# Gated linear attention in a two-layer trunk: one stacked product per chunk and head

## The chip, the cores and the metric

The kernel runs on one core of a Trainium2 chip. The metric is the device time of one execution in microseconds (us). Before the change the median of three runs is 723.94 us (723.78 to 724.06).

## The reference

Two layers over one sequence of 256 positions with 1024 features, in float32. Each layer multiplies by one wide matrix, gives the columns to three groups of heads, multiplies their joined outputs by `w_out`, normalises, and runs a mixture of experts (16 experts, 2 per token) with another normalisation. Groups B and C are softmax attentions with four heads of 64. Group A, which the change concerns, is gated linear attention: four heads, keys of 64, values of 128, and four chunks of 64 positions.

```
b = cumsum(log_a, axis=3)                     # within a chunk
q_dec = (q * 64 ** -0.5) * exp(b)
k_inv = k * exp(-b)
a = where(causal, einsum('bhnid,bhnjd->bhnij', q_dec, k_inv), 0)
o_intra = einsum('bhnij,bhnjv->bhniv', a, v)
kv = einsum('bhncd,bhncv->bhndv', k * exp(b_last - b), v)
S_in[n + 1] = decay[n] * S_in[n] + kv[n]      # S_in[0] = 0
o = o_intra + einsum('bhncd,bhndv->bhncv', q_dec, S_in)
o = rms_norm(o, norm_gain) * silu(g_out)
```

So per head and chunk the output is masked scores times values plus decayed queries times the state that the chunk starts with.

## The kernel before

The 256 positions are two tiles of 128 (`t`), each of two chunks. A layer's mixer begins with the projection `pj`: the transposed input and each weight tile are split into a high and a low half in a rounded format, and three products (`whi` with `hhi`, `wlo` with `hhi`, `whi` with `hlo`) are summed. ACT makes `whi`, DVE makes `wlo`. The column groups come in the order of `ORDER` (line 39): the indexer, values, `GV` (values and gate rank of the linear attention), queries and keys of the two softmax attentions, `GK`, and `GG`, the output gate. The out-projection `po` uses the same three-product form, with `mx` for the softmax attentions and `mxG` for the linear one; `OUT_ORDER` (line 40) puts the four row blocks of `mxG` last (42 products of them before the first normalisation begins).

The class `Order` with `_Lane` (from line 75 on) fixes the order of instructions while the program is built. It holds a clock for each engine, books every instruction with the duration that `_Lane.cost` returns, and runs generators: a generator yields the tiles that it waits for, or a number of PSUM banks that must be free, and goes on when the booked clock of TensorE has reached that point. In between, the backbone (projection and out-projection) fills TensorE. So another duration in `cost`, or another `yield`, moves instructions on every engine. There are eight PSUM banks; `bank` takes one and `od.free` gives it back. Weights come in a ring of 33 buffers through SP's DMA queue. `pieces.fill` makes `whi` and `wlo` a fixed number of tiles ahead.

The generators that the change edits:

- `decays` (line 862): copies the values of both tiles from PSUM to `gv` (ACT, four copies), makes the gate's cumulative sums and the exponentials `eb`, `enb`, `ebl`.
- `linear` (line 939): `qd` is the decayed queries, `enb` and `ebl` become the two decayed keys. For each tile: four products `aT` (keys by queries, 64 rows of contraction), and a masked copy into `aM`, which was zeroed. Four transposes of `ebl` through TensorE give `kd`, which one ACT copy evicts. For each of three chunks: four products `kv`, and the state `S` (ACT's copy for the first, DVE for the others). For each tile and head the output bank gets a product of `aM` with `gv` over 128 rows, and one or two products of `qd` with `S` over 64 rows. Then ACT squares, DVE sums (`ms`), POOL takes the power -0.5, and DVE multiplies (`og`).

Two generators that run beside these are not edited but are moved: `softmax_pv` (line 602) with the scores `sc`, their maxima on DVE, the exponentials `s_sb` on ACT, the division by `ri` on DVE, transposes `pT`, products `pv` and the split into `mx`; and `gated` (line 1072), which multiplies `og` by `sg` (silu of the gate, ACT), transposes it (`tr` from `og`), and evicts the high half (ACT) and the low half (DVE) of `mxG`. Every instruction goes through one helper, so nearly all rows carry one line, L235 in the kernel before and L237 in the changed one.

Of the kernel before, what the change touches and what calls it, by code (L numbers as in the profile page):

```python
# [17 lines left out]
P = 128  # L18
# [13 lines left out]
SENT = -3e38  # L32
THETA = 500000.0
TWO_PI = 2.0 * math.pi
CHUNKS = {"I": ([(3088, 584)], (1,) * 8, (292, 292)), "GV": ([(512, 528)], (1,) * 8, (264, 264)),
# [151 lines left out]
class _Lane:  # L187
# [3 lines left out]
    def cost(self, name, out, ins, kw, scalars=0):  # L191
        def free(a):
            n = 1
            for s in a.shape[1:]:
                n *= s
            return n
        n = free(out)
        psum = any(i.space == bass.MemoryType.PSUM for i in ins)
        if self.lane == "PE":
            if name == "transpose":  # L200
                return 110.0
            f = 1.68 if ins[0].dtype == F32 else 0.42
            c = max(214.0 if ins[0].dtype == F32 else 100.0, f * n)
            return c / 2 + 20 if out.shape[0] <= 64 and ins[0].shape[0] > 64 else c
        if self.lane == "ACT":
            return 0.833 * n + (52 if psum else 94) + 93 * (scalars + ("accum_out" in kw))
        if self.lane == "POOL":
            if name == "memset":
                return 0.8 * n + 70
            return 165.0 * n + 300 if kw.get("op") == OP.pow else 2.2 * n + 50  # L210
        m = max([n] + [free(a) for a in ins])
        if name == "reciprocal":
            return 6.3 * n + 68
        if name in ("tensor_scalar", "tensor_copy") and not psum:
            return 0.54 * n + 65 + 61 * scalars
        return 1.04 * m + 65 + 61 * scalars
# [23 lines left out]
def trunk_kernel(ctx, tc, x, positions, w_in, gate_up, gate_bias, norm_gain, w_out, ln_mix_g, ln_mix_b,  # L240
# [503 lines left out]
    for l in range(DEPTH):  # L744
# [114 lines left out]

        gl = {}  # L860

        def decays(ps):
            rT = t1("rT", (17, L))
            pool.memset(rT, 1.0)
            gv, ranks = [], []
            for t in range(NT):
                r_ = sm("rank", 16)
                act.activation(r_, ps[t][1][:, 248:264], AF.Copy)
                ranks.append(r_)
                gv.append(t2("gv"))  # L870
# [4 lines left out]
            gl["v"] = gv  # L875
            yield ranks
            yield 1
            b_ = bank("tr")
# [60 lines left out]
        def linear(bq, bk):  # L939
            while "decays" not in done:  # L940
                yield lambda: "decays" in done
            eb, enb, ebl = gl["e"]
            gv = gl["v"]
            gq, gk = (b.rearrange("p (a n) -> p a n", a=2) for b in (bq, bk))
            yield [bq, bk]
            dve.tensor_mul(enb, gk, enb)
            qd = t2("qd", (P, 2, L))
# [5 lines left out]
            yield [qd, enb]  # L953
            aM = t4("aM", (P, NT, 2, 2, P))
            pool.memset(aM, 0.0)
            for t in range(NT):
                ts = slice(t * P, (t + 1) * P)
                yield 2
                b_ = [bank("aT") for _ in range(2)]
                for hh in range(4):  # L960
                    r = slice(64 * (hh % 2), 64 * (hh % 2) + 64)
                    mm(b_[hh % 2].rearrange("p (h i) -> p h i", h=4)[:, hh // 2], enb[r, hh // 2, ts],
                       qd[r, hh // 2, ts])
                yield b_
                for s_ in range(2):
                    dve.copy_predicated(aM[:, t, s_], triu.bitcast(I32)[:, None, :].to_broadcast([P, 2, P]), b_[s_].rearrange("p (h i) -> p h i", h=4)[:, 0:2])
                od.free(*b_)
            yield ebl
            yield 1
            b_ = bank("kd")  # L970
            kdp = b_.rearrange("p (t n) -> p t n", t=NT)
            for t in range(NT):
# [4 lines left out]
            od.free(b_)  # L977
            yield kd
            S = []
            for c in range(3):  # L980
                yield 1
                b_ = bank("kv")
                kv = b_.rearrange("p (a n) -> p a n", a=4)
                u = slice(64 * (c % 2), 64 * (c % 2) + 64)
                for hh in range(4):
                    mm(kv[64 * (hh % 2):64 * (hh % 2) + 64, hh // 2], kd[u, c // 2, hh * 64:hh * 64 + 64],
                       gv[c // 2][u, hh * P:(hh + 1) * P])
                yield b_
                s = t1("S", (P, 2, P))
                if c == 0:  # L990
                    act.activation(s, kv[:, 0:2], AF.Copy)
                else:
                    for a in range(2):
                        dve.scalar_tensor_tensor(s[:, a], S[-1][:, a], eb[:, a, 64 * c + 63:64 * c + 64],
                                                 kv[:, a], op0=OP.mult, op1=OP.add)
                od.free(b_)
                S.append(s)
            for t in range(NT):
                yield ([S[0]], S[1:])[t]
                yield 2  # L1000
                bs = [bank("o") for _ in range(2)]
                b3 = [b.rearrange("p (h n) -> p h n", h=4)[:, 0:2] for b in bs]
                for hh in range(4):
                    r = slice(64 * (hh % 2), 64 * (hh % 2) + 64)
                    o_ = b3[hh % 2]
                    mm(o_[:, hh // 2], aM[:, t, hh % 2, hh // 2], gv[t][:, hh * P:(hh + 1) * P],
                       start=True, stop=False)
                    for u in range(2):
# [4 lines left out]
                sq = t2("sq", (P, 2, 2, P))  # L1013
                ms = sm("ms", 12)
                yield bs
                for s_ in range(2):
                    act.activation(sq[:, s_], b3[s_], AF.Square)
                yield sq
                dve.tensor_reduce(ms[:, 0:4].rearrange("p (a b) -> p a b", a=2), sq, AX.X, OP.add)
# [4 lines left out]
                for s_ in range(2):  # L1024
                    dve.tensor_mul(o[:, s_::2], b3[s_],
                                   ms[:, 8 + 2 * s_:10 + 2 * s_][:, :, None].to_broadcast([P, 2, P]))
                od.free(*bs)
                og.append(o)
            done.add("og")

# [662 lines left out]
```

## Time and profile before

| | us |
|---|---|
| median of three runs | 723.94 |
| the profiled execution | 723.8 |
| its span | 722.1 |
| TensorE (PE) busy | 692.0 (96%) |
| VectorE (DVE) busy | 440.7 (61%) |
| ScalarE (ACT) busy | 269.1 (37%) |
| GpSimd (POOL) busy | 44.0 (6%) |

The span runs from the first to the last instruction in the trace. PE's busy time counts products only; loads of weights (PEld) run beside them. An instruction of TensorE in float32 appears twice per product, a transpose once: `o<-S,qd ... x4` is two products. In a name such as `aT<-qd,enb` the tile left of the arrow is written, those right of it are read. Busy time of an engine that others wait for matters; idle time of the others does not.

### The profile page before, as it was taken

Reading aid. Unit: us, or ns where it says so; the run is one execution under the profiler, and the core shown is the slowest. Engines: PE = TensorE matmul, PEld = TensorE weight load, DVE = VectorE, ACT = ScalarE, POOL = GpSimd, SP = SyncE. Lnnn points to the kernel's source line nnn. Section 1 sums busy time; section 2 is a strip of 40 time slices with the busy share of each in tenths; the row PEclk is TensorE's granted clock in tenths of the full one; section 3 lists DMA queues with packets and bytes.
Section 4 is the critical chain, followed back from the end, with each engine's and each line's share of the span. In section 5 each row is a group of like instructions: output and inputs, shape, how many; then the busy total and the mean of one; then the engine's idle time right before and its main releaser. Section 6 shows DMA issues by size and latency. Waiting matters only on the chain. (4 is left out here: it accounts for less than half of the span.)

```text
span 722.1 us, 11110 instructions
## 1 busy us (share of the span) xinstructions
PE 692.0 (96%) x3817; PEld 400.0 (55%) x3817; DVE 440.7 (61%) x1115; ACT 269.1 (37%) x549; POOL 44.0 (6%) x72
## 2 busy tenths in 40 slices
PE   7999999999999989999899999999999999899993
PEld 6897977853533533533488889777435334343330
DVE  5897874660635445676488688757343546259645
ACT  5668646441312112212186666464223012022121
POOL 2000001010000001200130000011000000011002
PEclk9999999999999999999999999999999999999997
DMA  9899845879999999999999755469799999999971
GB/s 307 277 391 407 337 162 190 293 264 405 409 404 408 406 407 409 408 409 408 356 391 401 276 176 174 147 214 344 262 409 408 403 407 408 405 409 409 408 295 58
DMA packets 83245, 243.01 MB, mean 337 GB/s; under 512 B 10148, under 2 KB 14312, under 8 KB 83176
## 3 DMA queue, kind: packets, MB, share of 16 engines
q1 hardware_dynamic: 82504, 241.86, 88.0%
q8 instruction: 34, 0.56, 0.3%
q10 hardware_dynamic: 416, 0.26, 0.1%
q14 instruction: 35, 0.29, 0.1%
q0 software_dynamic: 256, 0.03, 0.0%
HBM read 241.08 MB, written 1.05 MB: 335 GB/s over the span
## 5 line engine op out<-in xcount | busy, mean ns | idle before, releaser
L235 PE MATMUL gu<-wf,xT 128*64 128x512 f32 x912 | 226.0, 594 | 3.7 <-PEq L1412 3.7
L235 PEld LDWEIGHTS gu<-wf,xT 128*64 128x64 f32 x912 | 71.8, 137 | 131.8 <-issue 124.1
L235 DVE SCALAR_TENSOR_TENSOR yt<-y,ws,yt 32x512 fp32r<-32x512 f32 (+1 forms) x116 | 86.7, 748 | 94.7 <-ACT yt L235 93.2
L235 DVE TENSOR_TENSOR wlo<-wf,whi 128x512 fp32r<-128x512 f32 (+2 forms) x174 | 97.3, 598 | 38.9 <-ACT whi L235 36.5
L235 PE MATMUL y<-wf,actT 128*64 128x512 f32 x432 | 110.5, 595 | 1.8 <-ACT actT L235 1.8
L235 ACT ACTIVATE whi<-wf 128x512 fp32r<-128x512 f32 (+2 forms) x176 | 86.7, 551 | 14.1 <-PE po L235 9.5
L235 PE MATMUL pj<-whi,hhi 128*128 128x512 f32 (+2 forms) x224 | 81.6, 364 | 0.0
L235 PE MATMUL pj<-wlo,hhi 128*128 128x512 f32 (+2 forms) x224 | 78.1, 349 | 1.7 <-DVE wlo L235 1.5
L235 PE MATMUL pj<-whi,hlo 128*128 128x512 f32 (+2 forms) x224 | 77.7, 347 | 0.0
L235 ACT ACTIVATE yt<-y,ws 128x512 fp32r<-128x512 f32 x60 | 36.9, 688 | 104.2 <-PE y L235 77.3
L235 PEld LDWEIGHTS y<-wf,actT 128*64 128x64 f32 x432 | 34.0, 137 | 54.1 <-issue 41.4
L235 DVE TENSOR_TENSOR act<-act,gu 128x512 f32<-128x512 f32 x16 | 11.0, 688 | 84.4 <-PE gu L235 62.8
L235 PE MATMUL gu<-wx,xT 128*64 128x512 f32 x112 | 52.7, 596 | 0.0
L235 PEld LDWEIGHTS pj<-whi,hhi 128*128 128x128 f32 x224 | 42.1, 188 | 8.3 <-issue 2.9
L235 PEld LDWEIGHTS pj<-wlo,hhi 128*128 128x128 f32 x224 | 42.1, 188 | 7.2 <-DVE wlo L235 3.5
L235 PEld LDWEIGHTS pj<-whi,hlo 128*128 128x128 f32 x224 | 42.0, 188 | 5.1
L235 ACT ACTIVATE actT<-aT 128x512 f32<-128x512 f32 x16 | 9.5, 595 | 85.8 <-PE aT L235 85.8
L235 ACT ACTIVATE xT<-xT,cols 128x256 f32<-128x256 f32 x32 | 17.4, 565 | 56.9 <-PE xT L235 56.9
L235 ACT ACTIVATE act<-gu 128x512 f32<-128x512 f32 x16 | 9.6, 597 | 76.4 <-PE gu L235 76.4
L235 PE MATMUL y<-wx,actT 128*64 128x512 f32 x80 | 33.4, 595 | 0.0
L235 DVE TENSOR_TENSOR z<-z,sc 128x512 f32<-128x512 f32 x48 | 29.7, 680 | 0.4 <-PE sc L235 0.4
L235 PE MATMUL sc<-yt,sT 128*128 128x512 f32 x72 | 23.8, 430 | 1.7 <-ACT yt L235 1.6
(269 smaller groups left out, 923.4 us busy)
## 6 DMA issues: line engine op xcount, KB each, us to landing
wf<-in_w_expert_gate_dram SPq DMA_DIRECT2D x114, 512.0 KB, 10.1
wf<-in_w_expert_up_dram SPq DMA_DIRECT2D x114, 512.0 KB, 10.0
wf<-in_w_expert_down_dram SPq DMA_DIRECT2D x108, 512.0 KB, 10.1
wf<-in_w_in_dram SPq DMA_DIRECT2D x32, 512.0 KB, 10.0
wx<-in_w_expert_down_dram SPq DMA_DIRECT2D x36, 256.0 KB, 5.8
wf<-in_w_out_dram SPq DMA_DIRECT2D x16, 512.0 KB, 10.5
wx<-in_w_expert_up_dram SPq DMA_DIRECT2D x24, 256.0 KB, 6.7
wx<-in_w_expert_gate_dram SPq DMA_DIRECT2D x10, 512.0 KB, 7.6
```

Of the source, the lines that this page charges most:

```text
L235: return fn(*a, **kw)
```

## The change

Scores and queries are stacked on the contraction rows, and so are values and states, so that a head's output in a chunk is one product over 128 rows. `X` holds, for head and chunk, the decayed queries in one half of the partitions and the masked scores in the other; `W[c]` holds the state of the chunk's start and the chunk's values in the matching halves. The halves change places between even and odd heads. The scores, `kd` and `kv` are made on 64 by 64 tiles, because they must land in the right half. The values' columns of `GV` are divided 256 and 272 in place of 264 and 264. `cost` gets one more rule for products on 64 by 64 tiles.

```diff
+            if out.shape[0] <= 64 and ins[0].shape[0] <= 64 and n <= 128:
+                return max(50.0, f * n / 2)
...
-                act.activation(gv[t][:, 0:264], ps[t][0][:, 0:264], AF.Copy)
-                act.activation(gv[t][:, 264:512], ps[t][1][:, 0:248], AF.Copy)
+            W = [t2("W", (P, 4, P)) for _ in range(4)]
+            pool.memset(W[0], 0.0)
+            for t in range(NT):
+                for u in range(2):
+                    for s_ in range(2):
+                        for a in range(2):
+                            act.activation(W[2 * t + u][half(1 - s_), 2 * a + s_], ps[t][a][half(u), s_ * P:(s_ + 1) * P], AF.Copy)
...
-            dve.scalar_tensor_tensor(qd, gq, 0.125, eb, op0=OP.mult, op1=OP.mult)
+            for s_ in range(2):
+                r = half(s_)
+                dve.scalar_tensor_tensor(X[r, s_::2].rearrange("p a c i -> p a (c i)"), gq[r], 0.125, eb[r], op0=OP.mult, op1=OP.mult)
...
+            for a in range(2):
+                for c in range(4):
+                    for s_ in range(2):
+                        mm(b4[s_][half(1 - s_), a, c], enb[half(s_), a, 64 * c:64 * c + 64], X[half(s_), 2 * a + s_, c])
+            yield bs
+            for s_ in range(2):
+                o = half(1 - s_)
+                dve.copy_predicated(X[o, s_::2], triu.bitcast(I32)[o, None, None, o].to_broadcast([64, 2, 4, 64]), b4[s_][o])
...
-            for t in range(NT):
                 for a in range(2):
-                    tr(kdp[:, t, a * P:(a + 1) * P], ebl[:, a, t * P:(t + 1) * P])
-            kd = t2("kd", (P, NT, 256))
-            act.activation(kd, kdp, AF.Copy)
+                    for s_ in range(2):
+                        mm(b4[s_][half(1 - s_), c, a], ebl[half(s_), a, 64 * c:64 * c + 64], ident[half(s_), half(s_)])
+                for s_ in range(2):
+                    act.activation(kd[c][half(1 - s_)], b4[s_][half(1 - s_), c], AF.Copy)
...
+                        mm(kv[s_][half(s_), a], kd[c][half(1 - s_), a], W[c][half(1 - s_), 2 * a + s_])
...
+                            dve.scalar_tensor_tensor(W[c + 1][r, 2 * a + s_], W[c][r, 2 * a + s_], eb[r, a, 64 * c + 63:64 * c + 64],
+                                                     kv[s_][r, a], op0=OP.mult, op1=OP.add)
...
-                    mm(o_[:, hh // 2], aM[:, t, hh % 2, hh // 2], gv[t][:, hh * P:(hh + 1) * P],
-                       start=True, stop=False)
                     for u in range(2):
-                        c = 2 * t + u
-                        if c:
-                            mm(o_[64 * u:64 * u + 64, hh // 2], qd[r, hh // 2, 64 * c:64 * c + 64],
-                               S[c - 1][r, hh // 2], start=False, stop=True)
+                        mm(b3[half(u), hh], X[:, hh, 2 * t + u], W[2 * t + u][:, hh])
...
+                act.activation(sq, b3, AF.Square)
...
+                dve.tensor_mul(o, b3, ms[:, 8:12, None].to_broadcast([P, 4, P]))
```

On TensorE, in layer 0, the output block of tile 1 stood between `pv` and the last projection products. Before:

```order
L235 MATMUL pT<-ident,s_sb 128x128 x8
L235 MATMUL pv<-pT,v 64x128 x12
L235 MATMUL o<-gv,aM 128x128
L235 MATMUL o<-S,qd 64x128 x2
L235 MATMUL o<-gv,aM 128x128
L235 MATMUL o<-S,qd 64x128 x2
L235 MATMUL o<-gv,aM 128x128
L235 MATMUL o<-S,qd 64x128 x2
L235 MATMUL o<-gv,aM 128x128
L235 MATMUL o<-S,qd 64x128 x2
```

and now, in the same place:

```order
L237 MATMUL pT<-ident,s_sb 128x128 x8
L237 MATMUL pv<-pT,v 64x128 x12
L237 MATMUL po<-whi,mx 128x512
L237 MATMUL po<-wlo,mx 128x512
L237 MATMUL po<-whi,mx 128x512 x2
L237 MATMUL po<-wlo,mx 128x512
L237 MATMUL po<-whi,mx 128x512
L237 MATMUL o<-W,X 64x128 x8
```

The twelve products of the block are eight of one form, and six products of the out-projection have come between it and `pv`.

On TensorE, in layer 1, near the end of the mixer, the transposes of `og` stood apart, among products of `po`. Before:

```order
L235 MATMUL po<-wlo,mx 128x512
L235 MATMUL po<-whi,mx 128x512
L235 MATMUL tr<-ident,og 128x128 x4
L235 MATMUL po<-whi,mx 128x512
L235 MATMUL po<-wlo,mx 128x512
L235 MATMUL po<-whi,mx 128x512 x2
L235 MATMUL po<-wlo,mx 128x512
L235 MATMUL po<-whi,mx 128x512
L235 MATMUL tr<-ident,og 128x128 x4
L235 MATMUL po<-whi,mx 128x512
```

and now:

```order
L237 MATMUL po<-wlo,mx 128x512
L237 MATMUL po<-whi,mx 128x512
L237 MATMUL tr<-ident,og 128x128 x8
L237 MATMUL pT<-ident,s_sb 128x128 x8
L237 MATMUL pv<-pT,v 64x128 x12
L237 MATMUL po<-whi,mx 128x512
L237 MATMUL po<-wlo,mx 128x512
```

The eight transposes stand together, and `pT` and `pv` of the second softmax tile, which stood ahead of the second `o` block before, stand right behind them.

On DVE, at the same place of layer 1, before:

```order
L235 TENSOR_REDUCE ms<-sq 128x4
L235 TENSOR_SCALAR ms<-ms 128x4
L235 TENSOR_TENSOR wlo<-wf,whi 128x512 x2
L235 TENSOR_TENSOR og<-o,ms 128x2x128 x2
L235 TENSOR_TENSOR og<-og,sg 128x512 x2
L235 TENSOR_TENSOR wlo<-wf,whi 128x512 x2
L235 SCALAR_TENSOR_TENSOR mxG<-tr,cols,mxG 128x4x128
L235 TENSOR_TENSOR wlo<-wf,whi 128x512
L235 SCALAR_TENSOR_TENSOR mxG<-tr,cols,mxG 128x4x128
```

and now (`ISA` is the maximum over a head's scores):

```order
L237 ISA s_sb,mx<-sc,acc 128x256
L237 ISA mx 128x1
L237 TENSOR_SCALAR mx<-mx 128x4
L237 TENSOR_TENSOR wlo<-wf,whi 128x512
L237 TENSOR_TENSOR og<-o,ms 128x512
L237 TENSOR_TENSOR og<-og,sg 128x512 x2
L237 SCALAR_TENSOR_TENSOR mxG<-tr,cols,mxG 128x4x128 x2
L237 RECIPROCAL ri<-mx 128x4
L237 TENSOR_SCALAR s_sb<-s_sb,ri 128x256 x4
L237 TENSOR_TENSOR mx<-pv,mx 128x512
```

The second softmax tile's maxima (four pairs of ISA rows, the last one shown) have come between the sum `ms` and `og`, and its scalings stand behind the two `mxG` evictions.

## Rows read from the trace of the kernel before

**Rows 1.** The page, busy us, share of the span and instructions of each engine.
```profile
PE 692.0 (96%) x3817; PEld 400.0 (55%) x3817; DVE 440.7 (61%) x1115; ACT 269.1 (37%) x549; POOL 44.0 (6%) x72
```
**Rows 2.** Windows: us, busy of PE, PEld, DVE, ACT, POOL, PEclk, DMA share, GB/s.
```profile
480.00:490.00 10.00, 10.00 (x50) 8.28 (x49) 8.03 (x14) 7.14 (x12) 0.00 (x0) 1.00 0.64 213
```
**Rows 3.** Waits of PE: us in total, times, longest us.
```profile
PE pj L235 <- DVE wlo L235: 1.5, 3, 0.7
```
**Rows 4.** Timeline of PE, layer 0: start us, us, what.
```profile
97.14 0.40 PE L235 MATMUL pj<-whi,hlo 128*128 128x512 f32 x1
97.47 0.71 PE L235 MATMUL aT<-qd,enb 64*128 64x128 f32 x8
...
98.45 0.39 PE L235 MATMUL pj<-wlo,hhi 128*128 128x512 f32 x1
98.68 0.40 PE L235 MATMUL pj<-whi,hlo 128*128 128x512 f32 x1
...
100.45 0.60 PE L235 MATMUL kd<-ident,ebl 128*128 128x128 f32 x4
...
102.36 0.65 PE L235 MATMUL kv<-gv,kd 64*64 64x128 f32 x8
```
**Rows 5.** Timeline of PE, layer 0, around the two output blocks.
```profile
107.22 0.40 PE L235 MATMUL pj<-whi,hlo 128*128 128x512 f32 x1
...
110.82 0.40 PE L235 MATMUL pj<-wlo,hhi 128*128 128x512 f32 x1
...
115.71 1.58 PE L235 MATMUL pv<-pT,v 128*64 128x128 f32 x24
117.22 0.49 PE L235 MATMUL o<-gv,aM 128*128 128x128 f32 x2
...
120.69 0.39 PE L235 MATMUL pj<-wlo,hhi 128*128 128x512 f32 x1
```
**Rows 6.** Timeline of PE, layer 1, transposes of the second softmax tile.
```profile
470.32 1.03 PE L235 MATMUL pT<-ident,s_sb 128*128 128x128 f32 x8
```
**Rows 7.** Timeline of ACT, value copies of layer 0, end of layer 1's mixer.
```profile
49.20 1.21 ACT L235 ACTIVATE gv<-pj 128x264 f32<-128x264 f32 x4
...
471.02 1.09 ACT L235 ACTIVATE pT<-pT 128x512 f32<-128x512 f32 x2 [2.54 <-PE pT L235]
472.95 0.60 ACT L235 ACTIVATE mx<-pv 128x512 fp32r<-128x512 f32 x1 [0.85 <-ACT pT L235]
...
482.16 0.69 ACT L235 ACTIVATE mxG<-tr,cols 128x512 fp32r<-128x512 f32 x1
```
**Rows 8.** Timeline of DVE, layer 1, end of the mixer.
```profile
461.81 0.42 DVE L235 CUSTOM_DVE_ANT_0 s_sb<-sc,acc 128x256 f32<-128x256 f32 x1 [1.71 <-PE sc L235]
...
466.75 0.17 DVE L235 RECIPROCAL ri<-mx 128x4 f32<-128x4 f32 x1
466.95 1.14 DVE L235 TENSOR_SCALAR s_sb<-s_sb,ri 128x256 f32<-128x256 f32 x4
...
476.54 0.69 DVE L235 TENSOR_REDUCE ms<-sq 128x4 f32<-128x512 f32 x1 [2.26 <-ACT sq L235]
...
477.46 0.69 DVE L235 TENSOR_TENSOR wlo<-wf,whi 128x512 fp32r<-128x512 f32 x1
...
479.44 0.75 DVE L235 TENSOR_TENSOR og<-o,ms 128x256 f32<-128x256 f32 x2
480.11 1.28 DVE L235 TENSOR_TENSOR og<-og,sg 128x512 f32<-128x512 f32 x2
...
482.89 0.75 DVE L235 SCALAR_TENSOR_TENSOR mxG<-tr,cols,mxG 128x512 fp32r<-128x512 f32 x1
```
**Rows 9.** Windows: a stop of PE, and the end of the span.
```profile
261.00:262.00 1.00, 0.00 (x0) 0.00 (x0) 0.00 (x0) 0.00 (x0) 0.00 (x0) 1.00 1.04 414
...
709.00:712.00 3.00, 1.46 (x4) 0.59 (x4) 2.12 (x5) 0.19 (x1) 0.15 (x1) 1.00 0.00 0
712.00:713.00 1.00, 0.00 (x0) 0.00 (x0) 0.93 (x5) 0.06 (x1) 0.55 (x2) 0.64 0.00 0
```

More of the change, by code (lines that the diff above doesn't have):

```diff
@@ L860, in trunk_kernel, with half @@
         gl = {}
+        def half(s):
+            return slice(64 * s, 64 * s + 64)
         def decays(ps):
@@ L942, in linear @@
             eb, enb, ebl = gl["e"]
-            gv = gl["v"]
+            W = gl["W"]
             gq, gk = (b.rearrange("p (a n) -> p a n", a=2) for b in (bq, bk))
+            X = t4("X", (P, 4, 4, 64))
+            for s_ in range(2):
+                pool.memset(X[half(1 - s_), s_::2], 0.0)
             yield [bq, bk]
             dve.tensor_mul(enb, gk, enb)
-            qd = t2("qd", (P, 2, L))
-            dve.scalar_tensor_tensor(qd, gq, 0.125, eb, op0=OP.mult, op1=OP.mult)
+            for s_ in range(2):
+                r = half(s_)
+                dve.scalar_tensor_tensor(X[r, s_::2].rearrange("p a c i -> p a (c i)"), gq[r], 0.125, eb[r], op0=OP.mult, op1=OP.mult)
             od.free(bq)
@@ L952, in linear @@
             od.free(bk)
-            yield [qd, enb]
-            aM = t4("aM", (P, NT, 2, 2, P))
-            pool.memset(aM, 0.0)
-            for t in range(NT):
-                ts = slice(t * P, (t + 1) * P)
-                yield 2
[L959 to L967, printed above, removed]
@@ L998, in linear @@
[L998 to L1005, printed above, removed]
-                    mm(o_[:, hh // 2], aM[:, t, hh % 2, hh // 2], gv[t][:, hh * P:(hh + 1) * P],
-                       start=True, stop=False)
-                    for u in range(2):
-                        c = 2 * t + u
-                        if c:
-                            mm(o_[64 * u:64 * u + 64, hh // 2], qd[r, hh // 2, 64 * c:64 * c + 64],
-                               S[c - 1][r, hh // 2], start=False, stop=True)
-                sq = t2("sq", (P, 2, 2, P))
-                ms = sm("ms", 12)
+            yield [X, enb]
@@ new lines, in linear @@
+            yield 2
+            bs = [bank("aT") for _ in range(2)]
+            b4 = [b.rearrange("p (a c i) -> p a c i", a=2, c=4) for b in bs]
+            for a in range(2):
[6 more added lines that the diff above has]
+                dve.copy_predicated(X[o, s_::2], triu.bitcast(I32)[o, None, None, o].to_broadcast([64, 2, 4, 64]), b4[s_][o])
@@ new lines, in linear @@
+            od.free(*bs)
+            yield ebl
+            yield 2
+            bs = [bank("kd") for _ in range(2)]
+            b4 = [b[:, 0:384].rearrange("p (c a d) -> p c a d", c=3, a=2) for b in bs]
+            kd = [t1("kd", (P, 2, 64)) for _ in range(3)]
+            for c in range(3):
+                for a in range(2):
+                    for s_ in range(2):
+                        mm(b4[s_][half(1 - s_), c, a], ebl[half(s_), a, 64 * c:64 * c + 64], ident[half(s_), half(s_)])
+                for s_ in range(2):
+                    act.activation(kd[c][half(1 - s_)], b4[s_][half(1 - s_), c], AF.Copy)
@@ L1015, in linear @@
+            od.free(*bs)
+            for c in range(3):
+                yield [kd[c], W[c]]
+                yield 2
+                bs = [bank("kv") for _ in range(2)]
+                kv = [b.rearrange("p (a n) -> p a n", a=4) for b in bs]
+                for a in range(2):
+                    for s_ in range(2):
+                        mm(kv[s_][half(s_), a], kd[c][half(1 - s_), a], W[c][half(1 - s_), 2 * a + s_])
                 yield bs
                 for s_ in range(2):
-                    act.activation(sq[:, s_], b3[s_], AF.Square)
+                    r = half(s_)
+                    if c == 0:
+                        act.activation(W[1][r, s_::2], kv[s_][r, 0:2], AF.Copy)
+                    else:
+                        for a in range(2):
+                            dve.scalar_tensor_tensor(W[c + 1][r, 2 * a + s_], W[c][r, 2 * a + s_], eb[r, a, 64 * c + 63:64 * c + 64],
+                                                     kv[s_][r, a], op0=OP.mult, op1=OP.add)
+                od.free(*bs)
@@ new lines, in linear @@
+            for t in range(NT):
+                yield [X] + W[2 * t:2 * t + 2]
+                yield 1
+                b_ = bank("o")
+                b3 = b_.rearrange("p (h n) -> p h n", h=4)
+                for hh in range(4):
+                    for u in range(2):
+                        mm(b3[half(u), hh], X[:, hh, 2 * t + u], W[2 * t + u][:, hh])
+                sq = t2("sq", (P, 4, P))
+                ms = sm("ms", 12)
+                yield b_
+                act.activation(sq, b3, AF.Square)
@@ L1018, in linear @@
                 yield sq
-                dve.tensor_reduce(ms[:, 0:4].rearrange("p (a b) -> p a b", a=2), sq, AX.X, OP.add)
+                dve.tensor_reduce(ms[:, 0:4], sq, AX.X, OP.add)
                 dve.tensor_scalar(ms[:, 4:8], ms[:, 0:4], 1.0 / P, RMS_EPS, op0=OP.mult, op1=OP.add)
@@ L1023, in linear @@
                 o = t2("og", (P, 4, P))
[L1024 to L1027, printed above, removed]
+                dve.tensor_mul(o, b3, ms[:, 8:12, None].to_broadcast([P, 4, P]))
+                od.free(b_)
                 og.append(o)
```

35 lines of the change are left out of this document (4 added, 31 removed).

## The prediction

> **What bounds the kernel now.** I read the page's busy shares first: TensorE (PE) is busy 692.0 of 722.1 us, and no other engine comes near [rows 1]. Then the busy time by windows, for the mixer: in 480:490 PE is busy all of its 10 us at clock 1.00, beside 8.03 us of VectorE (DVE) and 7.14 of ScalarE (ACT) [rows 2]; the windows around the linear attention read alike in both layers. The list of PE's waits has one entry that a mixer edit touches: 1.5 us in three waits for `wlo`, the low half of a weight, the longest 0.7 us [rows 3]. The timeline of PE then shows the blocks themselves without a gap. So the bound is PE's own instruction stream; work taken off it moves the end one for one, and so does every gap that opens in it. The MoE behind each mixer runs from PE as well and passes a shift on.
>
> **What PE sheds, per layer.** Projection products start 0.23 us apart (98.45 and 98.68). The first `aT` block: from the product at 97.14 to the second one behind it at 98.45 are 1.31 us, less two products at 0.23 is 0.85; two such blocks 1.7. The `kd` transposes have a row of 0.60, which overlaps its neighbours; I count 0.4 [rows 4]. Output block `o` of t=0: 107.22 to 110.82 is 3.60, less two products 3.1; of t=1: 117.22 to 120.69 less one is 3.2 [rows 5]. Together 1.7 + 0.4 + 6.3 = 8.4 us per layer.
>
> **What PE takes on, per layer.** (a) Scores `aT`: sixteen products on 64 by 64 tiles with 64 columns. The nearest row is `kv`: four such products with 128 columns, 0.65 us [rows 4], with the 0.14 by which a block costs more than its row (0.85 against 0.71 for `aT`) 0.8. Of its eight instructions in pairs at 0.11 us, 0.45 is streaming and 0.35 the change of tiling in and out. Sixteen products are sixteen pairs: 0.9 with half the columns, 1.75 if 64 columns cost as many as 128. So 1.2 to 2.1; I take 1.2. (b) `kd`: twelve products of the same shape, 1.0 (upper bound 1.7). Here PE stops twice for ACT, which empties each chunk's pair of banks with two copies of 64x128 before PE writes on. Four `gv` copies of 264 or 248 columns take 1.21 us, 0.27 from start to start [rows 7]; a copy of 128 columns lies between 0.15 and 0.27, with the latency of one (0.4 at most) a stop is 0.3 to 0.7; I take 0.6, so 1.2 for two. (c) `o`: eight products with all 128 rows and 64 output columns, twice. The row of that form is `pv`: 24 instructions in 1.51 us [rows 5], so sixteen in 1.0, with the change of tiling 1.23; twice 2.5. Sum 1.2 + 1.0 + 1.2 + 2.5 = 5.9. **PE sheds 2.5 us per layer** before anything waits.
>
> **What waits now, layer 0.** The sixteen ACT copies of `v` replace four: 16 times 0.15 to 0.27 against 1.21, 1.2 to 3.1 us more ahead of the weight halves `whi` in ACT's queue, and `wlo` on DVE and the projection products wait behind these. Cover is the pieces made ahead; without it all of it would show. Bounds 0 and 3.1; I take 0.7, the longest wait for `wlo` seen [rows 3]. Before, eighteen products of `po` stood between the last transposes of `og` and the first product that reads `mxG`; now the eight transposes stand directly ahead of it, and the ACT eviction of 0.69 us [rows 7] and the start of DVE's of 0.75 [rows 8] show: 0.9. `pv` is followed by `po` rather than by `o`, some 0.3 for the change of tiling. The score products and the second `o` block find their inputs ready. The other edits on DVE, ACT and POOL (zeroing, queries in two instructions, fewer masked copies, states written in halves) I cost at nothing, since projection products stand beside them; without these each would show with its own length, some 0.3 to 0.7 by the rows of like size [rows 7, 8]. SP issues the same weight transfers in the same order. Layer 0: -2.5 + 0.7 + 0.9 + 0.3 = -0.6; the `kv` blocks stand alone more often, +0.3. I take -0.3.
>
> **What waits now, layer 1.** The end of the mixer is put together differently. Everything of the second softmax (`pT`, `pv`) now stands behind the transposes of `og`, and 24 `po` products behind `pv`.
> First stop, before the `og` transposes. After `pT` of t=0 PE has eight score instructions with 256 columns (four pairs at twice 0.11, with the change of tiling 1.1) and twelve `po` products at 0.23 (2.8): 3.9 us. Beside it, from the same point: ACT's `pT` copy (0.5 after its start-up of 0.2; two take 1.09), the square over 512 columns (0.6 by the same row) [rows 7], then on DVE the reduce 0.7, a `wlo` 0.6, four score maxima of 0.42 that overlap a little (1.5), a `wlo` 0.6, `og` over 512 columns 0.65, the first `og` times `sg` 0.65 [rows 8], and 0.3 of small operations and hand-overs: 6.3. Stop 2.4 us. Without the maxima and the `wlo` in between it would be some 0.3; with a later ACT it grows one for one.
> Second stop, between those transposes and `pT` of t=1. DVE's queue has the two `mxG` evictions ahead of the reciprocal and the four scalings that `pT` reads. From the first four transposes: ACT's `mxG` 0.7 [rows 7], DVE's two 0.7 each, reciprocal 0.2, first scaling 0.35, hand-overs 0.2 [rows 8]: 2.8, less the 0.4 of the other transposes: 2.4 us. Before, the products of `po` stood there and nothing waited.
> Third, `po` behind `pv` needs `mx`: ACT's copy 0.60 [rows 7] with hand-overs 0.9, and 0.2 until DVE's half. Before, the second `o` block covered this.
> Behind them the 42 products on `mxG` find all ready. Layer 1: -2.5 + 2.4 + 2.4 + 1.1 = +3.4. Uncertainty of the three stops: 3 to 8 in all.
>
> **The clock.** It is 1.00 through the span but for the first microseconds and the tail. A PE that stood still through all of 261:262 left it at 1.00; at the tail, where four products in 709:712 were all the work, 1.46 us busy of 3, it was 0.64 in 712:713, the mean of a stretch at 2.4 and one at 1.2 GHz [rows 9]. Layer 1 would now have two stops of 2.4 us with one microsecond of transposes between: thinner than the tail before its fall. I think a fall to 1.2 GHz in the second stop likelier than not. Its least price is the eight `pT` transposes at half rate, 1.03 more [rows 6]; with `pv` too it is 2.5, and with as many `po` products as the kernel's other cold stretch, 4. I take 1.2.
> The Trainium skill, page "TensorE: Matmul & The Clock Gate", section "Why this matters for your kernels", says that idle gaps between bursts of products in the middle of a kernel send the clock back to its lower level; rows 9 show one gap that did not. [...]
>
> **Sum.** Profiled execution of before 723.8 us (span 722.1 and 1.7 around it); -0.3 + 3.4 + 1.2 = +4.3: 728.1. The median of the runs shown is 723.94, 0.14 above the profiled one; so 728.2.
> The same skill's page "TensorEngine Tiling (Array Packing)", section "PSUM Bottleneck", warns that after tiling the emptying of PSUM may become the bottleneck, and asks for evictions over many tiles at once; this change splits them. No row shows that here yet; by it the stops above are the lasting cost.
>
> **Rivals.**
> *The clock stays.* All waits as above, without 1.2: 727.0. For it speaks the gap at 261 us, against it the tail [rows 9].
> *The waits are hidden: faster.* The freed 2.5 us per layer reach the end, because the second `og` arrives in time. That needs ACT and DVE in layer 1 to run 2.4 us ahead of what I assume, ahead of the first stop, and the `mxG` evictions to be done before PE gets through its transposes. Deciding point: the first stop under 0.3 us. Then 723.9 - 5.0 + 1.9 of layer 0's waits + some 1 = 721.8. Against it: the order of DVE's queue is fixed in the program, and each of its durations is in a row.
> *The stops are half as long.* Layer 1 -2.5 + 3.0 = +0.5, layer 0 -0.3, the clock kept: 724.1, no change to be told.
> *Narrow products cost like wide ones.* `aT` 0.9 and `kd` 0.7 more in each layer (the upper bounds above), 3.2 in all, nothing of it hidden: 731.4 with the clock's fall, 730.2 without. For it: no row has 64 columns on TensorE in this form; against it, times of products follow columns from 128 to 512 in the rows.
> *The clock falls for longer.* Through `pv` and some `po`: 729.5 to 731.
>
> **How the numbers follow.** Forecast with the clock's short fall 0.34, clock kept 0.24, long fall 0.16, narrow products dear 0.10, half stops 0.09, faster 0.07. Each case has about 1 us of its own to either side. Leaving out the lowest tenth (faster, the edge of half stops) and the highest tenth: 725.0 to 731.5. About 0.2% (1.4 us) is what a measurement of this kernel can tell from no change: faster by more 0.07, within 0.10, slower 0.83.
>
> **What would show it.** In the changed kernel's trace: `aT` in one block of about 1.2 us and each `o` block of 1.2 where 3.1 stood; two gaps of PE of 2 to 3 us either side of eight `og` transposes in layer 1, the second released by DVE's scaled scores, and a third near 1 us behind `pv`; layer 0's mixer as long as before within 1 us; PEclk below 1.00 somewhere between the first gap and the `po` products behind it. The MoE stretches keep their length. I am wrong if the gaps in layer 1 stay under 2 us in sum, or if PE's blocks of narrow products take 2 us each; a mixer in layer 1 that is shorter than before refutes the forecast.

## The result and the profile after

The changed kernel takes 733.82 us (median of four runs, 732.62 to 735.40) against 723.86 for the kernel before (four runs, 723.38 to 724.06): ratio 1.0133, 95% interval 1.0119 to 1.0148. It is slower, as forecast, but by 10.0 us where 4.3 were forecast, and the time lies above the range.

The profiled execution of the changed kernel is the longest of the four, 735.4 us with a span of 733.7; it stands 11.6 us behind that of before. The page's busy row and the largest of PE's waits that a mixer can cause:

```profile
PE 695.3 (95%) x3873; PEld 402.7 (55%) x3873; DVE 444.4 (61%) x1117; ACT 278.1 (38%) x582; POOL 44.7 (6%) x76
```

```profile
PE tr L237 <- DVE og L237: 2.7, 1, 2.7
PE pT L237 <- DVE s_sb L237: 2.2, 1, 2.2
...
PE pj L237 <- DVE wlo L237: 1.8, 4, 0.8
...
PE kd L237 <- ACT kd L237: 1.2, 4, 0.4
...
PE gx L237 <- issue: 0.7, 1, 0.7
PE po L237 <- ACT mx L237: 0.7, 1, 0.7
...
PE po L237 <- ACT mxG L237: 0.3, 1, 0.3
```

Against [rows 1, 3]: PE is busy 3.3 us longer although the change takes work off it, since part of its work ran at half clock (below), and the first two waits are new. They are the two stops that the forecast named. On the timeline of PE at the end of layer 1's mixer (against [rows 6]):

```profile
480.23 0.39 PE L237 MATMUL po<-whi,mx 128*128 128x512 f32 x1
483.29 1.16 PE L237 MATMUL tr<-ident,og 128*128 128x128 f32 x8 [2.68 <-DVE og L237]
486.62 1.97 PE L237 MATMUL pT<-ident,s_sb 128*128 128x128 f32 x8 [2.16 <-DVE s_sb L237]
488.51 2.88 PE L237 MATMUL pv<-pT,v 128*64 128x128 f32 x24
492.08 0.50 PE L237 MATMUL po<-whi,mx 128*128 128x512 f32 x1 [0.69 <-ACT mx L237]
```

The eight `pT` take 1.97 us where they took 1.03, and the 24 `pv` instructions 2.88 where they took 1.58: near half rate. The windows show the clock there, and in two stretches that the forecast did not price, the routings between mixer and experts (columns as in [rows 2]):

```profile
149.00:150.00 1.00, 0.99 (x9) 0.76 (x8) 0.92 (x9) 0.47 (x3) 0.00 (x0) 1.00 1.04 383
150.00:151.00 1.00, 0.11 (x1) 0.00 (x0) 1.00 (x10) 1.00 (x1) 0.00 (x0) 0.87 1.06 387
151.00:152.00 1.00, 0.81 (x4) 0.84 (x5) 0.97 (x9) 0.14 (x1) 0.00 (x0) 0.50 1.06 389
...
157.00:158.00 1.00, 1.00 (x8) 1.00 (x7) 0.75 (x2) 0.72 (x2) 0.00 (x0) 0.72 0.00 0
...
482.00:483.00 1.00, 0.00 (x0) 0.00 (x0) 1.00 (x2) 1.00 (x5) 0.00 (x0) 1.00 0.20 25
...
486.00:487.00 1.00, 0.39 (x2) 0.39 (x3) 0.96 (x5) 0.73 (x2) 0.00 (x0) 0.50 0.59 221
...
517.00:518.00 1.00, 1.00 (x6) 0.94 (x6) 0.15 (x1) 0.00 (x0) 0.00 (x0) 0.50 0.29 119
```

PEclk, the column behind POOL, reads 0.50 (1.2 GHz) from 150.7 to 157.6, from 485.2 to 492.1 and from 516.0 to 519.4 us (the edges follow from the shares of the windows), and 1.00 between. The fall at 485 follows the stop of 2.7 us, the transposes and part of the second stop. The one at 150.7 lies in a wait of 1.08 us for DVE, behind idle products and one small product; the one at 516 lies just behind the same wait in layer 1. Both kernels have this wait. In layer 0, before and after:

```profile
151.59 1.18 PE L235 MATMUL xT<-G,h 128*128 128x128 f32 x8 [1.08 <-DVE top L235]
```

```profile
151.19 2.05 PE L237 MATMUL xT<-G,h 128*128 128x128 f32 x8 [1.08 <-DVE top L237]
```

The starts of the same instruction in both timelines show where the 11.6 us arose (`gu` is the experts' first product, `lgT` the routing's, `gq` the first of `GK`, `warm` idle products):

| until | before | after | behind | in the stretch |
|---|---|---|---|---|
| first `sc` of layer 0 | 71.61 | 71.73 | +0.12 | +0.97, less 0.85 (the clock rose at 7.4, not 9.1) |
| first `lgT` of layer 0 (mixer's end) | 146.11 | 145.72 | -0.39 | -0.51 |
| first `gu` of layer 0 | 155.65 | 158.12 | +2.47 | +2.86, routing, clock 0.50 |
| `warm` ahead of layer 1 | 356.78 | 358.93 | +2.15 | -0.32, experts |
| first `gq` of layer 1 | 432.72 | 435.82 | +3.10 | +0.95 |
| first `lgT` of layer 1 | 500.33 | 510.36 | +10.03 | +6.93 |
| first `gu` of layer 1 | 509.86 | 521.43 | +11.57 | +1.54, routing, clock 0.50 |

The blocks `aT` and `o` cost what was forecast, `kd` 0.5 us more. PE in layer 0, against [rows 4, 5]:

```profile
100.01 0.39 PE L237 MATMUL pj<-whi,hlo 128*128 128x512 f32 x1
100.33 1.15 PE L237 MATMUL aT<-X,enb 64*64 64x64 f32 x32
...
101.74 0.39 PE L237 MATMUL pj<-wlo,hhi 128*128 128x512 f32 x1
101.97 0.40 PE L237 MATMUL pj<-whi,hlo 128*128 128x512 f32 x1
102.30 0.45 PE L237 MATMUL kd<-ident,ebl 64*64 64x64 f32 x8
103.11 0.74 PE L237 MATMUL kd<-ident,ebl 64*64 64x64 f32 x8 [0.36 <-ACT kd L237]
104.10 0.74 PE L237 MATMUL kd<-ident,ebl 64*64 64x64 f32 x8 [0.26 <-ACT kd L237]
...
105.11 0.40 PE L237 MATMUL pj<-wlo,hhi 128*128 128x512 f32 x1
...
124.45 0.40 PE L237 MATMUL po<-whi,mx 128*128 128x512 f32 x1
124.78 1.09 PE L237 MATMUL o<-W,X 128*64 128x128 f32 x16
...
126.14 0.39 PE L237 MATMUL po<-wlo,mx 128*128 128x512 f32 x1
```

By the subtraction of [rows 4], `aT` costs 101.74 - 100.01 - 0.46 = 1.27, `kd` with its waits 105.11 - 101.97 - 0.46 = 2.68, an `o` block 126.14 - 124.45 - 0.46 = 1.23. Forecast: 1.2, 2.2, 1.23.

### The profile page after: what moved, and what is told of

Read it like the earlier page. It is cut to its first block, busy times and chain, and to the rows that moved or that the text cites. A ratio compares the mean times of both kernels' runs of the same rounds, so it can differ in the third digit from the quotient of the medians.

```text
span 733.7 us, 11273 instructions
## 1 busy us (share of the span) xinstructions
PE 695.3 (95%) x3873; PEld 402.7 (55%) x3873; DVE 444.4 (61%) x1117; ACT 278.1 (38%) x582; POOL 44.7 (6%) x76
## 5 line engine op out<-in xcount | busy, mean ns | idle before, releaser
L237 DVE TENSOR_TENSOR wlo<-wf,whi 128x512 fp32r<-128x512 f32 (+3 forms) x174 | 97.7, 598 | 49.0 <-ACT whi L237 41.8
L237 ACT ACTIVATE whi<-wf 128x512 fp32r<-128x512 f32 (+3 forms) x176 | 86.6, 552 | 14.2 <-PE po L237 7.4
L237 DVE TENSOR_SCALAR xT<-xT,cols 128x256 f32<-128x256 f32 x32 | 17.1, 544 | 16.1 <-ACT xT L237 15.7
```

Of the source, the lines that this page charges most:

```text
L237: return fn(*a, **kw)
```

## Why the order moved: the selection gate

The forecast took the new order of layer 1 as given. Its origin is on DVE. The second attention of each layer (`attend("S")`) needs a mask, which eight rounds of top-8 selection on DVE prepare. The line ahead of each round is `yield lambda: od.clk["DVE"] <= od.clk["PE"] + 400`: a round is issued only while DVE's booked clock is at most 400 ns ahead of TensorE's. The last instruction of the selection of layer 1's first tile (t=0), before and after:

```profile
449.67 0.29 DVE L235 TENSOR_TENSOR acc<-acc,mc 128x128 f32<-128x128 f32 x1
```

```profile
467.92 0.29 DVE L237 TENSOR_TENSOR acc<-acc,mc 128x128 f32<-128x128 f32 x1
468.81 0.72 PE L237 MATMUL sc<-qkT 64*128 64x128 f32 x8
```

It ends 18.25 us later, 3.10 of which the whole program had lost by then. So the scores `sc` come behind the first `o` block (467.79), and what follows them (softmax, `pT`, `pv`) lands behind the transposes of `og`. No run shows the booked clocks themselves. One thing that can push DVE's ahead, tested below in e5 and e8, is that it must wait for ACT, which has sixteen copies of `v` instead of four. ACT and DVE in layer 0 (against [rows 7] for the copies):

```profile
48.67 3.56 ACT L237 ACTIVATE W<-pj 64x128 f32<-64x128 f32 x16
```

```profile
53.09 1.46 DVE L237 TENSOR_TENSOR wlo<-wf,whi 128x512 fp32r<-128x512 f32 x2 [3.86 <-ACT whi L237]
```

The sixteen take 0.22 us each, 3.56 in place of 1.21; DVE waits 3.86 us for the weight's high half, where it waited 1.04 before.

## The experiments

Theory A: layer 1 lost its time because the gate put the selection off, and the stops and the clock's fall follow from that order. Rival B: the stops belong to the new blocks and their evictions, whatever the order. All twelve runs follow. "Median before" is that of the kernel before in the same session; ratio and interval are as recorded from the single runs and need not be the quotient of the two medians.

| run | median | median before | ratio, 95% interval |
|---|---|---|---|
| e1_gate | 723.75 | 724.24 | 0.9983, 0.9968 to 0.9997 |
| e2_held_before | 729.75 | 724.24 | 1.0076, 1.0055 to 1.0098 |
| e3_filled | 732.11 | 724.24 | 1.0115, 1.0091 to 1.0138 |
| e4_route | 733.49 | 724.24 | 1.0121, 1.0103 to 1.0140 |
| e5_pieces | 725.54 | 724.27 | 1.0025, 1.0012 to 1.0038 |
| e6_kd | 719.94 | 724.27 | 0.9937, 0.9921 to 0.9954 |
| e7_all | 719.99 | 724.27 | 0.9937, 0.9920 to 0.9953 |
| e8_shared | 726.19 | 724.27 | 1.0043, 1.0017 to 1.0068 |
| e9_gate_layer1 | 725.22 | 724.43 | 1.0003, 0.9987 to 1.0019 |
| e10_all_idle | 718.16 | 724.43 | 0.9896, 0.9864 to 0.9927 |
| e11_idle | 734.39 | 724.43 | 1.0122, 1.0090 to 1.0155 |
| e12_before_idle | 724.54 | 724.43 | 0.9986, 0.9969 to 1.0002 |

**e1_gate and e9_gate_layer1: the gate alone.**

```diff
-                    yield lambda: od.clk["DVE"] <= od.clk["PE"] + 400
+                    yield lambda: od.clk["DVE"] <= od.clk["PE"] + (400 if t else 900)         # e1
+                    yield lambda: od.clk["DVE"] <= od.clk["PE"] + (900 if l and not t else 400)  # e9
```

> The changed kernel with one number of the scheduler's changed: the steps of the top-8 selection for the first tile may be issued while DVE's booked clock is up to 900 ns ahead of TensorE's, not 400. Theory A (the selection of layer 1 came 15 us late because this gate shut, and everything behind it moved behind the linear attention): layer 1's two stops of 2.7 and 2.2 us are gone, the clock stays at 1.00 in its mixer, and the 2 to 2.5 us per layer that TensorE sheds come through: 719 to 722. Rival B (the stops belong to the new blocks and their evictions, whatever the order): both stops stay and the time stays at 732 to 735.

> The changed kernel with the gate at 900 for the first tile's selection of layer 1 alone; layer 0 keeps its order. Theory A: layer 0's mixer is as in the changed kernel, layer 1's is some 8 us shorter and without a fall of the clock, so 724 to 726.5. Rival: part of the gain of the run with the gate in both layers came from layer 0, and the stops of layer 1 stay: 731 to 734.

In e1 the selection's last instruction starts at 444.98, and PE at the end of layer 1's mixer reads:

```profile
469.93 1.04 PE L237 MATMUL pT<-ident,s_sb 128*128 128x128 f32 x8
...
481.70 0.60 PE L237 MATMUL tr<-ident,og 128*128 128x128 f32 x4
483.52 0.60 PE L237 MATMUL tr<-ident,og 128*128 128x128 f32 x4
```

No wait stands at either, and `pT` is ahead of the transposes again. By the starts, layer 1's mixer is 1.60 us shorter than before the change (433.13 to 499.14) where the changed kernel's is 6.93 longer: 8.5 us from one number, the clock's fall included. Layer 0's is 1.60 shorter (0.51 in the changed kernel). In e9 layer 0 keeps its 0.49 and layer 1 is again 1.59 shorter. Both stops are gone and the clock is kept in layer 1's mixer, as A expected, and B falls; but 1.6 us per layer came through, not the 2 to 2.5 that e1's expectation names. The medians of 723.75 and 725.22 are above e1's range of 719 to 722 and inside e9's: the stretches ahead of the mixers, with the copies of `v`, are still 1.0 us longer each, and in part of the executions the clock falls in a routing (e1's profile: 0.50 from 504.8 to 508.2, 1.54 us). The four executions of e1 at a mean clock of 0.994 took 721.34 to 722.41 us, the six at 0.991 took 723.44 to 725.36.

**e2_held_before: the late selection without the change.**

```diff
-                    yield lambda: od.clk["DVE"] <= od.clk["PE"] + 400
+                    yield lambda: od.clk["DVE"] <= od.clk["PE"] + (400 if t or l == 0 else -1000)
```

> The kernel before, nothing stacked, with the same gate held back in layer 1 alone (DVE's booked clock must be 1000 ns behind TensorE's). Theory A: the selection ends late here too, the second attention's scores move behind the linear attention, and gaps of TensorE open at the end of layer 1's mixer without any of the new products: 727 to 729. Rival B: no new gap, 723 to 725.

The kernel before, with its own products, loses 5.5 us in the median. In its profile the selection's last instruction starts at 468.63 and layer 1's mixer is 4.69 us longer; the longest of the waits that open at its end:

```profile
473.73 0.92 PE L235 MATMUL pT<-ident,s_sb 128*128 128x128 f32 x4 [0.42 <-DVE s_sb L235]
...
481.70 0.49 PE L235 MATMUL po<-whi,mx 128*128 128x512 f32 x1 [0.50 <-ACT whi L235]
482.43 0.50 PE L235 MATMUL po<-wlo,mx 128*128 128x512 f32 x1 [0.23 <-DVE wlo L235]
...
487.75 0.50 PE L235 MATMUL po<-whi,mx 128*128 128x512 f32 x1 [0.71 <-ACT mx L235]
```

So a selection as late as the changed kernel's suffices for a longer mixer without any of the new products. With two waits of 0.2 and 0.3 the new waits sum to 2.4 us; the rest of the 4.69 was not separated, and the two stops of over 2 us are not among them: the late selection alone does not make these. The price is above the 727 to 729 expected, and 1.53 us of the profiled run is a fall of the clock in layer 0's routing.

**e3_filled: what the clock costs in layer 1.** `warm(6)` is twelve products of the identity that nobody reads.

```diff
+                if l == 1 and t == 0:
+                    yield 1
+                    warm(6)
                 yield og[t]
...
+            if gap and t == 1:      # gap: the second attention of layer 1
+                yield 1
+                warm(6)
```

> The changed kernel with 12 idle products (results unused) ahead of the transposes of og and 12 ahead of pT in layer 1, as much as fills the two stops. Theory A (the stops cost their own length, and the fall of the clock in them 2.3 us more): the clock stays at 1.00 through the end of layer 1's mixer and the time falls by 2 to 3 us against the changed kernel, to 730.5 to 732. Rival C (the clock's fall is the larger part of what was lost): it falls by 5 us or more. If the clock falls all the same, the fill does not count as work for it.

```profile
479.51 0.39 PE L237 MATMUL po<-whi,mx 128*128 128x512 f32 x1
479.74 2.84 PE L237 MATMUL warm<-ones,ident 128*128 128x128 f32 x24
482.50 1.26 PE L237 MATMUL tr<-ident,og 128*128 128x128 f32 x8
483.59 2.84 PE L237 MATMUL warm<-ones,ident 128*128 128x128 f32 x24
486.27 1.04 PE L237 MATMUL pT<-ident,s_sb 128*128 128x128 f32 x8
```

`pT` is back at 1.04 us, the granted clock is 1.00 up to 722 us but for a fall in layer 0's routing, and layer 1's mixer is 5.04 us longer than before in place of 6.93: 1.9 less. The fill has a price of its own: from the last `po` to `pT` are 6.76 us (479.51 to 486.27) where the changed kernel took 6.39 (480.23 to 486.62), 0.4 more. So the clock's fall there is worth some 2.3 us and the order 4.7. The median fell by 1.7 us against the changed kernel's 733.82, less than the 2 to 3 expected; rival C, which wanted 5 or more, falls.

**e5_pieces and e8_shared: the sixteen copies.**

```diff
-                act.activation(gv[t][:, 0:264], ps[t][0][:, 0:264], AF.Copy)        # e5, in the kernel before
-                act.activation(gv[t][:, 264:512], ps[t][1][:, 0:248], AF.Copy)
+                for r0 in (0, 64):
+                    for c0, n, a in ((0, 132, 0), (132, 132, 0), (264, 124, 1), (388, 124, 1)):
+                        act.activation(gv[t][r0:r0 + 64, c0:c0 + n], ps[t][a][r0:r0 + 64, c0 - 264 * a:c0 - 264 * a + n], AF.Copy)
...
+                            if u:                                                   # e8, in the changed kernel
+                                dve.tensor_copy(o_, i_)
+                            else:
+                                act.activation(o_, i_, AF.Copy)
```

> The kernel before with its four value copies per layer written as sixteen of 64 rows and 124 or 132 columns, nothing else changed. Theory A1 (the sixteen copies cost about 1 us of waits in each layer, and through the booked clocks they move the selection and the scores too): the first layer's scores start 0.8 to 1.2 us later than before, and the second attention's scores of layer 1 stand behind the linear attention's first products; 724 to 727. Rival (the copies are hidden, the 1 us comes from the other edits): no shift of the scores, 723.5 to 724.5.

> The changed kernel with the value copies shared between ACT and DVE and nothing else; the gate stays at 400. Theory A2 (the order of layer 1 tips by small differences of the booked clocks, and the sixteen copies on ACT are one of the things that tipped it): the selection ends in time, the two stops are gone and the time is 720 to 724. Rival (the gate alone decides, whatever ACT does): the stops stay, 731 to 734.

In e5 the last instruction of layer 1's selection starts at 459.83, ten microseconds late, though no product of the kernel is changed. Its scores (460.45) still stand ahead of the first `o` block (462.48), and layer 1's mixer is 0.15 us shorter than before: a lateness of ten microseconds costs nothing here. The shift of the first scores, +0.39 us with a clock that rose 0.48 us earlier (worth 0.24), is below the 0.8 to 1.2 expected, and the stretch ahead of layer 1's mixer is 0.23 us longer. So of the 0.97 and 0.95 us that the changed kernel lost in these stretches the sixteen copies alone explain some 0.6 and 0.2. Another 0.2 in each layer is the projection of `GV`, now in pieces of 256 and 272 columns: 12.16 us for 11.95 in layer 0 and 11.73 for 11.52 in layer 1. The rest was not separated. The median of e5 is 1.3 us above before; its profile has a fall of the clock in layer 0's routing, 1.53 us, so this is not the copies' price. In e8 the selection's last instruction starts at 450.83 with the gate still at 400, both stops are gone, and layer 1's mixer is 0.92 us shorter than before. The median of 726.19 lies above the 720 to 724 expected: the `kd` stops grew to 2.1 us in four, and the clock fell behind those of layer 0 (0.50 from 104.2 to 107.6) and in the routing. So the copies are one of the things that shut the gate. Sharing them did not shorten the stretch ahead of the mixer (in layer 1 it is 1.29 us longer than before, 0.95 in the changed kernel); it gave back the order. How much of the rest is due to TensorE's shorter booked times stays open.

**e6_kd, e7_all, e10_all_idle: the saving brought home.** All products of `kd` ahead of their copies (e6, with e1's gate); with them the copies shared and the gate at 1600 (e7); with them four idle products in each routing's wait (e10).

```diff
             for c in range(3):
                 for a in range(2):
                     for s_ in range(2):
                         mm(b4[s_][half(1 - s_), c, a], ebl[half(s_), a, 64 * c:64 * c + 64], ident[half(s_), half(s_)])
+            for c in range(3):
                 for s_ in range(2):
                     act.activation(kd[c][half(1 - s_)], b4[s_][half(1 - s_), c], AF.Copy)
...
                 slots(G[:, 0], 0, 0)
+                warm(2)             # e10, e11, e12
```

> The run with the gate at 900, and the kd products of all three chunks ahead of their six ACT copies, so that TensorE no longer stops twice for ACT there. Theory A: the two stops of 0.36 and 0.26 us with their 0.3 of hand-over go in each layer, 1.2 to 2.4 us less than with the gate alone (723.75): 721.5 to 722.5. Rival: the stops return as a wait of kv for the copies, 723 to 724.

> Gate at 1600, kd products ahead of their copies, and the value copies shared: the chunk of even number on ACT, the other on DVE. If the gate, the kd stops and the sixteen copies are what ate the saving, this gives 1 to 2 us per layer over the kernel before and a mixer without a fall of the clock: 717 to 721, faster than both. If the copies on DVE delay the low weight halves as much as they relieve ACT: 721 to 723.

> Gate at 1600, kd products ahead of their copies, value copies shared between ACT and DVE, and four idle products in the 1.1 us in which TensorE waits in each routing for DVE's gather matrix. If the fall of the clock in the routing of layer 1 (1.55 us in the run without them) comes from that idling, the clock stays at 1.00 from start to tail and the time is 718 to 719, faster than every version so far. If the fill only delays: 720 to 721.

In e6 the 24 `kd` instructions stand in one row of 0.91 us and PE does not wait there. Layer 0's mixer is 2.30 us shorter than before the change and layer 1's 3.12, against 1.60 each in e1: 2.2 us, as expected. The median fell by 3.8, more than expected: e6's profile has no fall of the clock in a routing and e1's has one of 1.54 us. The section "PSUM Bottleneck" of the Trainium skill's page "TensorEngine Tiling (Array Packing)" holds for `kd`: what limited the block was its emptying (2.68 us for 0.9 of products). e7 gained nothing over e6 in the median: its layer 0 mixer is 1.7 us shorter than e6's, and its profile lost 1.55 us to the clock at 501.0 to 504.4. With idle products there (e10) the clock is 1.00 from 8.7 to 708.4 us; two stretches of layer 1's mixer:

```profile
440.00:460.00 20.00, 20.00 (x192) 16.22 (x191) 14.48 (x43) 13.89 (x43) 1.04 (x2) 1.00 0.50 159
460.00:480.00 20.00, 20.00 (x138) 15.74 (x137) 14.33 (x32) 11.50 (x22) 2.42 (x2) 1.00 0.68 236
```

PE is busy all 40 us of these windows. e10 takes 718.16 us, inside the 718 to 719 expected, 1.0% less than before by the recorded ratio (0.9% by the medians) and 2.1% less than the changed kernel's median.

**e4_route, e11_idle, e12_before_idle: the clock in the routings.** e4 has `N_WARM = 5` in place of 2, ahead of the routing's small product; e11 and e12 have the four idle products of e10 in the changed kernel and in the kernel before.

> The changed kernel with ten idle products in place of four in front of the routing of both layers, where the changed kernel's trace shows the clock at 0.50 for 6.8 and 3.4 us. They push the routing back by some 0.6 us each. If the falls there are a fixed part of what was lost, the clock stays at 1.00 in the routing and the time falls by 2.9 + 1.6 - 1.2 = 3 us or so, to 730 to 731.5. If the falls come only in some executions, the median falls by less than 2 us.

> The changed kernel with the same four idle products in each routing and nothing else. Theory: the falls of the clock in the two routings are worth 1.5 to 4.4 us where they come, the rest of the loss is layer 1's mixer: 730 to 732.5 with a smaller spread. Rival (falls there are rare): 733 to 734.

> The kernel before with the same four idle products in each routing: the control. If the kernel before loses the clock there in some executions only, its median stays within 0.7 us and its highest run comes down to under 724.8. Rival (it never falls there before the change): no difference at all in any run.

In none of the three profiles does the clock fall in a routing. e4 pays 0.9 us per layer for it and ends 0.3 us under the changed kernel's median, as its expectation has it for falls that come in some executions only. Its 733.49 less the 1.8 paid is 731.7, an estimate of the changed kernel with the clock kept in both routings: by it the falls there are worth some 2.1 us in the median, where the profiled execution lost 4.4. In e11 the median stayed at 734.39, above both ranges expected: the profiled run, the shortest at 732.08, keeps the fall of layer 1's mixer (483.1 to 489.9) and has a new one at 411.4 to 414.8, behind PE's wait of 0.7 us for the gate ranks (`gx`), and the other three have a lower mean clock (0.984 against 0.987). So the total does not follow from filling one gap. e12 bears on whose the routing's falls are: its ten runs lie between 724.02 and 725.19 at mean clocks of 0.993 to 0.995, while seven of the nineteen runs of the kernel before beside it took 726.0 to 727.6 at 0.987 to 0.989. In the two sessions ahead of it, one run of thirteen and one of fourteen were like these seven. No trace of the kernel before shows such a fall; that it loses the clock in a routing too, in some executions, is concluded from the runs that the idle products rid of it, and from the falls at 151.4 and 152.0 us in e2 and e5, which have its products. The three runs shown ahead of the prediction, 723.78 to 724.06 us, give no sign of it.

## Why the prediction was right or wrong

- **What bounds the kernel: right.** Every microsecond lost in a mixer came out at the end; the experts' stretch changed by 0.3 us.
- **What PE sheds and takes on: right but for `kd`.** `aT` 1.27 and `o` 1.23 against 1.2 and 1.23. `kd` cost 2.68 against 2.2, waits included. The price of 64 columns in `aT` was near the lower bound, as taken; the rival of dear narrow products falls.
- **Copies of v: too small, and missing in layer 1.** 0.7 us was taken, in layer 0 alone; the stretches with the copies lost 0.97 and 0.95, of which e5 gives the copies some 0.6 and 0.2. In layer 1 it is not `wlo` that waits most but `gx`, 0.7 us: ACT's copy of the transposed gate ranks, which `gx` reads, stands behind the sixteen copies. The bounds, 0 to 3.1, held.
- **Layer 0's other steps:** -1.0 was the sum without the copies, -0.5 was measured; the 0.5 that `kd` cost more is the difference.
- **Layer 1's stops: the right places and engines, the size too small.** 2.68, 2.16 and 0.69 us were found for 2.4, 2.4 and 0.9. But "+3.4" for the layer is some 4.7 with the clock kept (e3). Of the 1.3 missed, `kd` is 0.5 and the first stop 0.4 (480.23 to 483.29, less a product of 0.23, is 2.8); the rest is spread over small waits that were not separated.
- **The clock: the failed step.** "I take 1.2" for the second stop was some 2.3, since `pv` fell under it as well as `pT`, as in the rival of a long fall. And the step ended there: the sum holds no price for the routings, where the profiled run lost 2.86 and 1.54 us. The profile of before, one execution, showed 1.00 there, and the text took it for a property of the kernel; e12's runs speak for one of the execution. The sentence on idle gaps that the prediction cites from the Trainium skill (page "TensorE: Matmul & The Clock Gate", section "Why this matters for your kernels") fits the fall behind the stop of 2.68 us; it does not tell the routings apart, where the same wait of 1.08 us left the clock at 1.00 in the profile of before and not in that of the changed kernel.
- **What the miss is made of.** The profiled execution lost 11.6 us where 4.3 were forecast. Of the 7.3 between, the routings are 4.4, the order of layer 1's mixer 1.3, the clock in it 1.1 and the stretch ahead of it 0.95; layer 0 and the experts give 0.4 back. So the clock's term failed by 5.5 us and layer 1's sum by 2.2, copies included. In this the clock's early rise at the start, 0.85 us, is luck of the execution. The profiled execution is the longest of the four; for the median, 5.6 us above the forecast, e4's estimate leaves 2.1 to the routings and 3.5 to the rest. Why the clock fell in a routing in one execution and not in another stays open.
- **The rivals.** "The waits are hidden" was set aside because DVE's order is fixed in the program. It is, but by a rule with a threshold: 400 to 900 gives that rival's layer 1 without stops, with 1.6 of its 2.5 us. Nothing in the rows showed it; the place to look was the reason for the moved `sc`, not only its cost.
- **The signs named beforehand** for the mixers were all seen, the third gap with 0.69 us. "The MoE stretches keep their length" held for the experts (0.3 us shorter) and failed for the routings ahead of them.

## What to carry to other kernels

When a change takes time off the bounding engine, ask first what the scheduler does with the time: here a gate of 400 ns between two booked clocks turned a saving of 1.6 us in layer 1's mixer into a loss of 6.9, and one number gave it back. When a block of instructions turns up in another place of the order, find the condition that moved it before pricing the gaps around it. Compare the granted clock over several executions, not one, before calling a stretch safe. Idle products inside a wait can keep the clock at no cost: in e12 each routing grew by 0.03 to 0.04 us.

## What the runs showed of the hardware that was not expected

The granted clock fell to 0.50 around a wait of 1.08 us in a routing: at 150.7 us, 0.6 us into the wait, behind a microsecond in which PE worked for 0.99 us (149 to 150). The profile of before has the same wait and kept 1.00. Where it fell in a routing it stayed at 0.50 for 3.4 or 6.8 us, and the `xT` products ran at near half rate (8 instructions 2.05 us, 1.18 in the kernel before). By the mean clocks, one and the same kernel lost it in some executions and not in others. Twelve idle products in each of the two stops of layer 1 held it at 1.00 there (e3's profile).
